# Group softmax on one core: 12 in-place tiles, one DMA ring that alternates store(i) and load(i+10)

## The chip, the cores and the metric

The kernel runs on one core of a Trainium2 chip. The core's engines used here are VectorE (DVE), ScalarE (ACT) and SyncE (SP, which issues the DMAs); TensorE is not used. Times are device microseconds of that core. The metric is the median time of one execution: 1601.17 us before, over three runs (1600.88 to 1601.21).

## What is computed

The input x has the shape (4, 4096, 4352), float32. Each row of 4352 values is cut into 8 groups of 544, and each group is replaced by its softmax.

```python
x_g = x.reshape(B, N, G, Dg)            # G = 8, Dg = 544
x_g = x_g - x_g.max(axis=-1, keepdims=True)
exp = np.exp(x_g)
out = exp / exp.sum(axis=-1, keepdims=True)
```

The whole input is read once from HBM and the whole output is written once: 285.21 MB each way.

## The kernel before

The 16384 rows are taken in 128 tiles of 128 rows, one row to a partition, so a tile is 128 x 4352 float32 values, 2176 KB (17408 bytes in each partition). For each tile the kernel

- loads it into xt with one DMA (line 32, issued by SyncE);
- takes the negated maximum of each of the 8 groups on VectorE (line 35, one reduction over the whole tile, into mx);
- computes the exponentials on ScalarE, one instruction per group (line 40), from xt into a second tile ot, with the group's sum going to a column of sm. The profile shows each as an ACTIVATE and a short ACTIVATION_READ_ACCUMULATOR;
- takes the reciprocals of the 8 sums on VectorE (line 49, into rs);
- multiplies each group by its reciprocal on VectorE (line 51), from ot into ot;
- stores ot with one DMA (line 52, issued by SyncE).

xt and ot come from one pool with bufs=4: four buffers for each of the two names. mx, sm and rs come from a small pool, also with four buffers each. The loop is written tile after tile; the framework schedules the instructions itself, so the order on an engine need not be the written one, and it puts in the semaphore waits. Each engine, and SyncE's queue of DMA issues, works its instructions in order: an instruction that waits holds those behind it on the same engine. All loads and stores are issued by SyncE and go through one DMA queue, q1, in the order of issue.

Of the kernel before, what the change touches and what calls it, by code (L numbers as in the profile page):

```python
# [1 line left out]

# [4 lines left out]


@with_exitstack
def kernel(  # L10
    ctx: ExitStack,
    tc: tile.TileContext,
    x: bass.AP,
    out: bass.AP,
):
    nc = tc.nc
    G = 8
    P = 128
    xf = x.flatten_outer_dims()
    of = out.flatten_outer_dims()  # L20
    N, D = xf.shape
    Dg = D // G
    xg = xf.rearrange("n (g d) -> n g d", g=G)
    og = of.rearrange("n (g d) -> n g d", g=G)
    ntiles = N // P

    pool = ctx.enter_context(tc.tile_pool(name="io", bufs=4))
    small = ctx.enter_context(tc.tile_pool(name="small", bufs=4))

    for t in range(ntiles):  # L30
        xt = pool.tile([P, G, Dg], mybir.dt.float32)
        nc.sync.dma_start(out=xt, in_=xg[t * P:(t + 1) * P])  # L32

        mx = small.tile([P, G], mybir.dt.float32)
        nc.vector.reduce_max(out=mx, in_=xt, axis=mybir.AxisListType.X, negate=True)  # L35

        sm = small.tile([P, G], mybir.dt.float32)
        ot = pool.tile([P, G, Dg], mybir.dt.float32)
        for g in range(G):
            nc.scalar.activation(  # L40
                out=ot[:, g, :],
                in_=xt[:, g, :],
                func=mybir.ActivationFunctionType.Exp,
                bias=mx[:, g:g + 1],
                scale=1.0,
                accum_out=sm[:, g:g + 1],
            )
        rs = small.tile([P, G], mybir.dt.float32)
        nc.vector.reciprocal(out=rs, in_=sm)  # L49
        for g in range(G):  # L50
            nc.vector.tensor_scalar_mul(out=ot[:, g, :], in0=ot[:, g, :], scalar1=rs[:, g:g + 1])  # L51
        nc.sync.dma_start(out=og[t * P:(t + 1) * P], in_=ot)  # L52


# [1 line left out]
_INS = ['x']  # L56
_OUTS = [((4, 4096, 4352), 'float32')]


# [23 lines left out]
```

## Time and profile before

| | |
|---|---|
| median of three runs | 1601.17 us |
| span of the profiled execution | 1599.5 us |
| moved between HBM and SBUF | 285.21 MB read, 285.21 MB written |
| mean over the span | 357 GB/s |
| VectorE busy | 1048.2 us, 66% |
| ScalarE busy | 760.8 us, 48% |
| DMA queue q1, time of its packets as a share of 16 engines' span | 85.6% |

The span runs from the first to the last instruction of the profiled execution; the time of a run lies a little above it. Busy shares are means over the whole span. Where an engine is idle, the profile names what released it, which says what it had been waiting for. SyncE computes nothing; its rows are DMA issues, and the time to landing of a DMA counts from its issue to the last arrival of its completion signals, so it includes the time that the transfer stands in the queue behind others. The rows on which the prediction rests stand in a section of their own below.

### The profile page before, as it was taken

What the parts mean: (1) busy time and instruction counts of PE and PEld (TensorE: products, weight loads), DVE (VectorE), ACT (ScalarE), POOL (GpSimd) and SP (SyncE); (2) the same over time, 40 slices, a digit from 0 to 9 for tenths busy, and PEclk for the clock granted to TensorE, in tenths of its full rate; (3) what the DMA queues carried; (4) which work ended last, traced back from release to release, by engine and by line L of the source; (5) the groups of instructions that cost most, each with busy time, mean ns of one, the idle gap of its engine ahead of it and who ended that gap; (6) DMA issues with size and microseconds to landing.
All of it is one profiled execution on the core that took longest, in us unless ns stands there. A gap on an engine that the chain in (4) does not pass through costs nothing.

```text
span 1599.5 us, 4255 instructions
## 1 busy us (share of the span) xinstructions
DVE 1048.2 (66%) x1280; ACT 760.8 (48%) x2049; POOL 0.2 (0%) x4
## 2 busy tenths in 40 slices
DVE  7568655587556775567765677656776567765566
ACT  6245444455444554445544355443554435544354
POOL 0000000000000000000000000000000000000000
DMA  8888998888988889888898888998889988898887
GB/s 362 355 341 349 376 383 346 337 349 369 390 348 341 349 355 390 361 337 353 351 383 369 341 349 355 374 378 336 344 359 376 376 342 341 362 375 371 344 340 312
DMA packets 36897, 570.71 MB, mean 357 GB/s; under 512 B 4096, under 2 KB 4096, under 8 KB 4096
## 3 DMA queue, kind: packets, MB, share of 16 engines
q1 hardware_dynamic: 36864, 570.44, 85.6%
q14 instruction: 33, 0.27, 0.0%
HBM read 285.21 MB, written 285.21 MB: 357 GB/s over the span
## 4 chain that ended last, share of the span: by engine, by line
DMA 33%; DVE 27%; ACT 26%; issue 10%; SPq 1%; DVEq 0%; ACTq 0%
DMA xt<-in_x_dram 33%; ACT ot L40 26%; DVE ot L51 18%; DVE mx L35 8%; DVE rs L49 1%; SPq L32 1%; SPq L52 1%; DVEq L78 0%; ACTq L78 0%
## 5 line engine op out<-in xcount | busy, mean ns | idle before, releaser
L40 ACT ACTIVATE ot<-xt,mx 128x544 f32<-128x544 f32 x1024 | 750.7, 734 | 817.8 <-DVE mx L35 667.3
L35 DVE TENSOR_REDUCE mx<-xt 128x8 f32<-128x4352 f32 x128 | 599.5, 4683 | 426.0 <-DMA xt<-in_x_dram 426.0
L51 DVE TENSOR_SCALAR ot<-ot,rs 128x544 f32<-128x544 f32 x1024 | 434.3, 499 | 4.5
L40 ACT ACTIVATION_READ_ACCUMULATOR ot<-xt,mx 128x1 f32 x1024 | 191.4, 187 | 0.0
L49 DVE RECIPROCAL rs<-sm 128x8 f32<-128x8 f32 x128 | 25.5, 199 | 113.3 <-ACT ot L40 113.3
L40 ACT ACT_TABLE_LOAD x1 | 1.3, 1283 | 9.7 <-DMA xt<-in_x_dram 9.7
L67 POOL MEMSET const-uint8-127<- 128x1 uint8 x1 | 0.1, 102 | 0.0
L67 POOL MEMSET const-bfloat16-1.0<- 128x1 bf16 x1 | 0.1, 101 | 0.0
L67 POOL MEMSET const-float32-0.0<- 128x1 f32 x1 | 0.1, 98 | 0.2 <-issue 0.2
L67 POOL MEMSET const-float32-1.0<- 128x1 f32 x1 | 0.1, 98 | 0.0
## 6 DMA issues: line engine op xcount, KB each, us to landing
xt<-in_x_dram SPq DMA_DIRECT2D x128, 2176.0 KB, 17.1
out_dram<-ot SPq DMA_DIRECT2D x128, 2176.0 KB, 6.6
```

The source lines that it names most:

```text
L32: nc.sync.dma_start(out=xt, in_=xg[t * P:(t + 1) * P])
L35: nc.vector.reduce_max(out=mx, in_=xt, axis=mybir.AxisListType.X, negate=True)
L40: nc.scalar.activation(out=ot[:, g, :], in_=xt[:, g, :], func=mybir.ActivationFunctionType.Exp, bias=mx[:, g:g + 1], scale=1.0, accum_out= ...
L49: nc.vector.reciprocal(out=rs, in_=sm)
L51: nc.vector.tensor_scalar_mul(out=ot[:, g, :], in0=ot[:, g, :], scalar1=rs[:, g:g + 1])
L52: nc.sync.dma_start(out=og[t * P:(t + 1) * P], in_=ot)
L67: nc = _bacc.Bacc("TRN2", target_bir_lowering=False, num_devices=1)
```

## The change

Three things are changed together. The second tile ot is gone: the exponentials and the multiplies work in place in xt. The pool has 12 buffers of that one tile. And the instructions are issued in the written order on each engine, which is now: ten loads first; then, for each i, the maximum and the exponentials of tile i, the reciprocals and multiplies of tile i-1, the store of tile i-1, and the load of tile i+9. So on SyncE store(j) is followed by load(j+10). With 12 buffers, load(j+10) goes into the buffer that tile j-2 had.

```diff
+    NBUF = 12
-    pool = ctx.enter_context(tc.tile_pool(name="io", bufs=4))
+    pool = ctx.enter_context(tc.tile_pool(name="io", bufs=NBUF))
     small = ctx.enter_context(tc.tile_pool(name="small", bufs=4))
-    for t in range(ntiles):
-        xt = pool.tile([P, G, Dg], mybir.dt.float32)
-        nc.sync.dma_start(out=xt, in_=xg[t * P:(t + 1) * P])
+    def load(i):
+        xt = pool.tile([P, G, Dg], f32, name="xt")
+        tiles[i] = xt
+        nc.sync.dma_start(out=xt, in_=xg[i * P:(i + 1) * P])
+    def store(i, eng):
+        eng.dma_start(out=og[i * P:(i + 1) * P], in_=tiles.pop(i))
+    def expo(i):
+        xt = tiles[i]
+        mx = small.tile([P, G], f32, name="mx")
         nc.vector.reduce_max(out=mx, in_=xt, axis=mybir.AxisListType.X, negate=True)
-        ot = pool.tile([P, G, Dg], mybir.dt.float32)
+        sm = small.tile([P, G], f32, name="sm")
+        sums[i] = sm
         for g in range(G):
             nc.scalar.activation(
-                out=ot[:, g, :],
+                out=xt[:, g, :],
                 in_=xt[:, g, :],
                 func=mybir.ActivationFunctionType.Exp,
                 bias=mx[:, g:g + 1],
                 scale=1.0,
                 accum_out=sm[:, g:g + 1],
             )
+    def scale(i):
+        xt = tiles[i]
+        rs = small.tile([P, G], f32, name="rs")
+        nc.vector.reciprocal(out=rs, in_=sums.pop(i))
         for g in range(G):
-            nc.vector.tensor_scalar_mul(out=ot[:, g, :], in0=ot[:, g, :], scalar1=rs[:, g:g + 1])
-        nc.sync.dma_start(out=og[t * P:(t + 1) * P], in_=ot)
+            nc.vector.tensor_scalar_mul(out=xt[:, g, :], in0=xt[:, g, :], scalar1=rs[:, g:g + 1])
+    AHEAD = NBUF - 2
+    with tc.manual_schedule():
+        for i in range(AHEAD):
+            load(i)
+        for i in range(nt + 1):
+            if i < nt:
+                expo(i)
+            if i:
+                scale(i - 1)
+                store(i - 1, nc.sync)
+                if i - 1 + AHEAD < nt:
+                    load(i - 1 + AHEAD)
```

## Rows read from the trace of the kernel before

**Rows 1.** The page: its first line, the packets' total, and part 3, DMA queue q1.
```profile
span 1599.5 us, 4255 instructions
...
DMA packets 36897, 570.71 MB, mean 357 GB/s; under 512 B 4096, under 2 KB 4096, under 8 KB 4096
...
q1 hardware_dynamic: 36864, 570.44, 85.6%
```

**Rows 2.** Groups by line: line, engine, operation, shapes, count | busy us, mean ns | idle before.
```profile
L40 ACT ACTIVATE ot<-xt,mx 128x544 f32<-128x544 f32 x1024 | 750.7, 734 | 817.8 <-DVE mx L35 667.3 <-issue 150.6
L35 DVE TENSOR_REDUCE mx<-xt 128x8 f32<-128x4352 f32 x128 | 599.5, 4683 | 426.0 <-DMA xt<-in_x_dram 426.0
L51 DVE TENSOR_SCALAR ot<-ot,rs 128x544 f32<-128x544 f32 x1024 | 434.3, 499 | 4.5
...
L49 DVE RECIPROCAL rs<-sm 128x8 f32<-128x8 f32 x128 | 25.5, 199 | 113.3 <-ACT ot L40 113.3
```

**Rows 3.** Waits, all engines: who waited for whom, us in total, times, longest.
```profile
DVE mx L35 <- DMA xt<-in_x_dram: 426.0, 64, 13.2
```

**Rows 4.** Waits of SyncE's queue, same columns.
```profile
SPq L52 <- DVE ot L51: 1397.0, 127, 24.1
```

**Rows 5.** Timeline of SyncE, 100 to 210 us: start, length, line, operation, count.
```profile
108.59 3.96 SPq L32 DMA_DIRECT2D xt<-in_x_dram  x4
135.47 22.77 SPq L52 DMA_DIRECT2D out_dram<-ot  x4
158.33 3.96 SPq L32 DMA_DIRECT2D xt<-in_x_dram  x4
```

**Rows 6.** Windows of 2 us: window, length, engines' busy, PEclk, DMA share, GB/s.
```profile
192.00:194.00 2.00, 2.00 (x5) 2.00 (x7) 0.00 (x0) 1.00 0.00 0
200.00:202.00 2.00, 1.44 (x4) 2.00 (x7) 0.00 (x0) 1.00 0.00 0
206.00:208.00 2.00, 1.61 (x4) 0.00 (x0) 0.00 (x0) 1.00 0.66 279
```

**Rows 7.** Longer windows: one with a turn in 24 us; loads; stores; loads; two turns.
```profile
160.00:184.00 24.00, 11.80 (x9) 8.46 (x23) 0.00 (x0) 1.00 1.01 418
...
166.00:184.00 18.00, 11.80 (x9) 8.46 (x23) 0.00 (x0) 1.00 1.01 431
...
37.40:53.00 15.60, 10.91 (x17) 7.26 (x21) 0.00 (x0) 1.00 1.01 429
4.00:22.00 18.00, 10.94 (x7) 8.88 (x22) 0.00 (x0) 1.00 1.00 428
...
161.00:167.00 6.00, 0.00 (x0) 0.00 (x0) 0.00 (x0) 1.00 0.98 360
...
260.50:266.50 6.00, 0.00 (x0) 0.00 (x0) 0.00 (x0) 1.00 1.00 367
```

**Rows 8.** Issue to landing: page's median store; issues at 0.73, 2.11, 58.47, 111.35 us.
```profile
out_dram<-ot SPq DMA_DIRECT2D x128, 2176.0 KB, 6.6
...
xt<-in_x_dram SPq DMA_DIRECT2D x1, 2176.0 KB, 8.9
...
xt<-in_x_dram SPq DMA_DIRECT2D x1, 2176.0 KB, 23.1
...
out_dram<-ot SPq DMA_DIRECT2D x1, 2176.0 KB, 7.6
...
xt<-in_x_dram SPq DMA_DIRECT2D x1, 2176.0 KB, 25.5
```

**Rows 9.** Timeline of SyncE, single issues: the first four loads, their fourth, a later fourth, the last store.
```profile
0.73 2.80 SPq L32 DMA_DIRECT2D xt<-in_x_dram  x4
2.11 1.42 SPq L32 DMA_DIRECT2D xt<-in_x_dram  x1
111.35 1.20 SPq L32 DMA_DIRECT2D xt<-in_x_dram  x1
1592.08 0.33 SPq L52 DMA_DIRECT2D out_dram<-ot  x1
```

More of the change, by code (lines that the diff above doesn't have):

```diff
@@ L24 @@
     og = of.rearrange("n (g d) -> n g d", g=G)
-    ntiles = N // P
-    pool = ctx.enter_context(tc.tile_pool(name="io", bufs=4))
+    nt = N // P
+    pool = ctx.enter_context(tc.tile_pool(name="io", bufs=NBUF))
     small = ctx.enter_context(tc.tile_pool(name="small", bufs=4))
-    for t in range(ntiles):
-        xt = pool.tile([P, G, Dg], mybir.dt.float32)
-        nc.sync.dma_start(out=xt, in_=xg[t * P:(t + 1) * P])
-        mx = small.tile([P, G], mybir.dt.float32)
+    f32 = mybir.dt.float32
+    tiles = {}
+    sums = {}
+    def load(i):
[7 more added lines that the diff above has]
+        mx = small.tile([P, G], f32, name="mx")
         nc.vector.reduce_max(out=mx, in_=xt, axis=mybir.AxisListType.X, negate=True)
-        sm = small.tile([P, G], mybir.dt.float32)
-        ot = pool.tile([P, G, Dg], mybir.dt.float32)
+        sm = small.tile([P, G], f32, name="sm")
+        sums[i] = sm
         for g in range(G):
             nc.scalar.activation(
-                out=ot[:, g, :],
+                out=xt[:, g, :],
                 in_=xt[:, g, :],
@@ L47 @@
             )
-        rs = small.tile([P, G], mybir.dt.float32)
-        nc.vector.reciprocal(out=rs, in_=sm)
+    def scale(i):
+        xt = tiles[i]
+        rs = small.tile([P, G], f32, name="rs")
+        nc.vector.reciprocal(out=rs, in_=sums.pop(i))
         for g in range(G):
-            nc.vector.tensor_scalar_mul(out=ot[:, g, :], in0=ot[:, g, :], scalar1=rs[:, g:g + 1])
-        nc.sync.dma_start(out=og[t * P:(t + 1) * P], in_=ot)
+            nc.vector.tensor_scalar_mul(out=xt[:, g, :], in0=xt[:, g, :], scalar1=rs[:, g:g + 1])
[11 more added lines that the diff above has]
+                    load(i - 1 + AHEAD)
 _INS = ['x']
```

## The prediction, made before the change was run

> **What bounds the kernel now.** I read the page's totals first. The span is 1599.5 us, 570.7 MB move in it at a mean of 357 GB/s, and the transfers' packets fill 85.6% of the span [rows 1]. No engine is near that: over 128 tiles VectorE needs (599.5 + 434.3 + 25.5)/128 = 8.28 us a tile and ScalarE 750.7/128 = 5.86 us [rows 2], while the kernel takes 1599.5/128 = 12.50 us a tile. So the DMA engines set the pace, and the question is what they do in the 14.4% in which they hold no packet.
>
> Second, who waits. VectorE waits 426.0 us, in 64 waits, for loads [rows 3]: two per group of four tiles. SyncE's queue waits 1397.0 us, in 127 waits, for the multiplies of line 51 [rows 4]. That queue holds everything behind a waiting store, the next loads too, and its timeline shows what this makes: four stores spread over 22.77 us, then four loads together, with a period of 158.33 - 108.59 = 49.74 us for four tiles [rows 5]. While the stores trickle out as VectorE finishes them, nothing else is queued: 0 GB/s in 192 to 194 and in 200 to 202 us, 279 in 206 to 208 [rows 6]. The holes are in the transfer queue, not in its speed.
>
> Third, what the transfers do when something is queued. Loads back to back run at 428 and 431 GB/s (the second with both engines at work), three stores back to back at 429 [rows 7]. A transfer is 2176 KB = 2.228 MB, so a load takes 2.228/431 = 5.17 us and a store 2.228/429 = 5.19 us. One thing costs more: the turn from a store to the load behind it. The 6 us around a turn run at 360 and 367 GB/s; against 430 that loses 6 x 70/430 = 0.98 and 6 x 63/430 = 0.88 us. The 24 us with a turn near its start run at 418 and lose 24 x 12/430 = 0.67 us [rows 7]. The landings agree: a store with loads behind it lands 7.6 us after its issue, the median store after 6.6 [rows 8].
>
> **The change part by part.** *Loads ahead and the ring's order.* Ten loads are issued at once; then SyncE issues store(j), load(j+10) in turn. Load(j+10) takes the buffer of tile j-2, so it waits until store(j-2) has landed. At that moment load(j+8), store(j-1), load(j+9) and store(j) are still queued, some 22 us of transfers. Behind the waiting load on SyncE stands store(j+1), and nobody but the transfer queue waits for these two. An issue takes 0.3 to 1.4 us (1.42 and 1.20 are the slow ones [rows 9]), and even a load on an idle queue lands in 8.9 us [rows 8], so the backlog covers the wait; the holes go.
>
> *The compute order.* scale(i-1) now stands behind max(i) on VectorE, and max(i) waits for load(i). So store(i-1) is ready about 4.7 (max) + 0.2 + 434.3/128 = 3.4, together 8.3 us, after load(i) lands. When load(i) lands, the queue's next store is store(i-9): eight stores, each 10 us or more apart, lie between. This costs nothing as long as VectorE's 8.28 us and ScalarE's 5.86 us a tile [rows 2] stay under a tile's transfer time, below. At the start store(0) is ready at 0.73 + 8.9 [rows 8, 9] + 4.7 + 5.9 + 3.6 = 24 us, and loads keep the queue busy to 56 us. At the end tile 127 needs 4.7 + 5.9 + 3.6 = 14.2 us after its load, and some 50 us of stores stand ahead of its store.
>
> *In place.* ot goes; the exponentials write over xt. No row shows an exponential in place. The nearest is line 51, which already works in place, ot on ot, at 499 ns for 544 columns [rows 2]. I take no change. ScalarE would have to slow from 5.86 to over 11 us a tile before it counted.
>
> *The turns.* This is the unknown. Before, there is one store-to-load turn per four tiles; now there is one per tile, 118 in all, and as many from load to store. For store to load I take 0.9 us, with 0.67 and 1.0 as its ends (three of the four rows lie at 0.88 to 1.0). For load to store the one near thing is a store issued at 135.47, just before the last load of its group landed at 111.35 + 25.5 = 136.85. That store landed at 135.47 + 6.6 = 142.07, 5.22 us behind the load [rows 5, 8, 9]: a store's own 5.19, so the turn cost nothing. I take 0. Its far end is the other turn's 0.9. On the low side both turns could vanish; less than no cost would mean over 431 GB/s, which no long stretch shows.
>
> *The sum, against the profiled span.* The fourth load lands at 2.11 + 23.1 = 25.2 us [rows 8, 9], and six more at 5.17 bring the tenth to 56.2. Then 118 pairs of 5.19 + 5.17 + 0.9 = 11.26 us give 1328.7. Ten last stores at 5.19 give 51.9. The last store's issue at 1592.08 plus 6.6 leaves 0.8 us to the end of the span [rows 8, 9]. Together 1437.6 us. The median of the runs, 1601.17, is 1.7 us above the profiled span, so the forecast is 1439.3. Against the period now: 49.74 us for four tiles becomes 45.0; some 7 us of holes go and three more turns take 2.7 back.
>
> [...]
>
> **The rivals.** *The forecast*: turns of 0.67 to 1.1 us a pair, 1412 to 1463 us (118 x 0.23 = 27 us down, 118 x 0.2 = 24 us up). 0.68.
>
> *Cheaper turns.* With reads and writes queued all the time the DMA engines could drift apart and cover the turns. With none at all a pair is 10.36 us and the time 1333; so 1333 to 1412. Against it: the loads are issued right behind their store (135.47 + 22.77 = 158.24, then 158.33 [rows 5]), some 5 us before the turn comes, and it still costs 0.9. 0.12.
>
> *Turns both ways.* If load to store costs as much as store to load, a pair is 12.16 us and the time 1546; so 1463 to 1546. The one row near it speaks against it. 0.10.
>
> *A ceiling on the mixed rate, no change.* If the mean of now, 357 GB/s, were all that both directions together can have, filling holes would only stretch the transfers: 570.4 MB at 357 GB/s is 1598 us, with the 1.7 about 1599. The long windows at 429 to 431, each in one direction, speak against it; that none is mixed leaves it open. [...] 0.04.
>
> *The queue runs dry, slower.* If the wait of a load falls on the store issued just ahead of it, rather than two stores back, whatever makes it so (the buffer's release, the count of transfers in flight), the change doesn't do what it says. Then the ring is empty whenever a load is issued: a load on an idle queue takes 8.9 us to land [rows 8], the store behind it 5.19, a pair 14.1 us, the time about 1774. It decides from a pair of (1599.5 - 108.9)/118 = 12.63 us on. Against it: the buffer distance of two in the loop, with 22 us of backlog against 8.9. 0.06. [...]
>
> **How the numbers follow.** The likeliest is 1439 us. Its own range is 1412 to 1463. To hold 8 in 10 the range takes the nearer parts of both neighbours, 1385 to 1510 (a turn of 0.45 us a pair at one end, 1.5 at the other), and leaves out the far parts of the neighbours, the ceiling and the dry queue. A difference of 0.2%, 3 us, is about what a measurement of this kernel can tell from none. Faster: 0.68 + 0.12 + 0.10 = 0.90; same 0.04; slower 0.06.
>
> **What the profile after would show.** DMA packets over 95% of the span and no 2 us window without bytes between 3 us and the end; a mean near 397 GB/s; SyncE's queue waiting for landings of stores where it now waits for line 51; a store landing about every 11.3 us. If the holes are gone and the period is 10.4 or 12.2 instead, the turns are mis-sized; at 12.5 with full packets the ceiling holds. Holes behind each store, with loads landing 9 us after issue, would make the step on the wait wrong. Exponentials well over 734 ns, or multiplies over 499, would make the in-place step wrong.

## The result, and the profile after

The changed kernel takes 1341.13 us (median, 1340.14 to 1341.88) against 1601.15 for the kernel before: a ratio of 0.8376, 95% interval 0.8364 to 0.8388. The forecast was 1439 with a range of 1385 to 1510. The direction was right, the gain was 260 us where 162 were forecast, and the time lies below the range, beside the low end (1333) of the rival "cheaper turns", which had 0.12.

The page of the changed kernel: its first line, the engines' busy times, the packets' total, and the DMA queue (compare [rows 1]).

```profile
span 1340.1 us, 4119 instructions
...
DVE 1046.7 (78%) x1280; ACT 764.3 (57%) x2049; POOL 0.2 (0%) x4
...
DMA packets 36896, 570.70 MB, mean 426 GB/s; under 512 B 4096, under 2 KB 4096, under 8 KB 4096
...
q1 hardware_dynamic: 36864, 570.44, 99.4%
q14 instruction: 32, 0.26, 0.0%
```

The same bytes fill 99.4% of the span instead of 85.6%. The busy times of VectorE and ScalarE are those of before. By these shares the time without a packet falls from 230 us to 8, and the time of the packets themselves from 1369 us to 1332: of the 259 us that the span lost, some 222 are holes and some 37 are packets that now take less time. The groups by line (compare [rows 2]) and SyncE's queue (compare [rows 4]) of the changed kernel:

```profile
L49 ACT ACTIVATE xt<-xt,mx 128x544 f32<-128x544 f32 x1024 | 751.2, 735 | 524.3 <-issue 435.8
L45 DVE TENSOR_REDUCE mx<-xt 128x8 f32<-128x4352 f32 x128 | 599.6, 4685 | 247.6 <-DMA xt<-in_x_dram 247.6
L63 DVE TENSOR_SCALAR xt<-xt,rs 128x544 f32<-128x544 f32 x1024 | 434.2, 498 | 4.5
...
SPq L37 <- DMA out_dram<-xt: 1104.5, 116, 16.7
```

Working in place costs nothing: 735 ns against 734, 498 against 499. SyncE now waits 1104.5 us, in 116 waits, at a load (line 37) for the landing of a store, where it used to wait 1397.0 us at a store for VectorE. The timeline of its issues in mid-run (start, length, operation):

```profile
499.26 0.33 SPq L37 DMA_DIRECT2D xt<-in_x_dram  x1
499.64 0.48 SPq L40 DMA_DIRECT2D out_dram<-xt  x1
509.55 0.33 SPq L37 DMA_DIRECT2D xt<-in_x_dram  x1
```

A pair takes 10.29 us here. That is less than the forecast's 11.26, and no more than the 10.36 that a load of 5.17 and a store of 5.19 need with no turn between them. Windows of the changed kernel say the same (window, length, engines' busy, PEclk, DMA share, GB/s): the first turn from the ten loads to the stores, the stretch behind it, mid-run, and the end.

```profile
52.00:58.00 6.00, 5.96 (x11) 4.73 (x13) 0.00 (x0) 1.00 0.99 408
...
56.00:62.00 6.00, 5.96 (x6) 3.83 (x11) 0.00 (x0) 1.00 1.02 437
...
400.00:600.00 200.00, 157.38 (x191) 114.14 (x308) 0.00 (x0) 1.00 1.01 431
...
1300.00:1325.00 25.00, 2.17 (x6) 0.00 (x0) 0.00 (x0) 1.00 1.00 428
1325.00:1330.00 5.00, 0.00 (x0) 0.00 (x0) 0.00 (x0) 1.00 0.24 101
1330.00:1335.00 5.00, 0.00 (x0) 0.00 (x0) 0.00 (x0) 1.00 0.19 80
1335.00:1340.00 5.00, 0.00 (x0) 0.00 (x0) 0.00 (x0) 1.00 0.08 35
```

Only the first turn shows: 408 against 431 over 6 us is 0.3 us. Windows this short swing by some packets (56 to 62 us has 437, 62 to 68 has 418). The completion signals agree: every transfer here sends sixteen (the 4096 packets under 512 B, for 256 transfers), which I read as one from each of the sixteen DMA engines; the records do not name the engine. By the median of the sixteen the tenth load and the first store together took 10.7 us, and the next two pairs 10.4 and 10.3. From the second turn on a mixed stream runs at 430 to 431 GB/s, the rate of loads alone in [rows 7]. And there is an end that the prediction had not: from 1326 us on only four of the sixteen DMA engines still work, three of them until 1335, the last until 1339.

So two questions stand: why a turn that cost 0.9 us before costs nothing now, and which parts of the change bring the gain.

### The profile page after: what moved, and what is told of

The parts are those of the page before. It is cut to its first block, busy times and chain, and to the rows that moved or that the text cites. A ratio compares the mean times of both kernels' runs of the same rounds, so it can differ in the third digit from the quotient of the medians.

```text
span 1340.1 us, 4119 instructions
## 1 busy us (share of the span) xinstructions
DVE 1046.7 (78%) x1280; ACT 764.3 (57%) x2049; POOL 0.2 (0%) x4
## 2 busy tenths in 40 slices
DMA packets 36896, 570.70 MB, mean 426 GB/s; under 512 B 4096, under 2 KB 4096, under 8 KB 4096
## 3 DMA queue, kind: packets, MB, share of 16 engines
q1 hardware_dynamic: 36864, 570.44, 99.4%
## 4 chain that ended last, share of the span: by engine, by line
DMA 88%; DVE 7%; SPq 1%; ACT 1%; issue 1%; DVEq 0%; ACTq 0%
DMA out_dram<-xt 85%; DVE mx L45 4%; DVE xt L63 3%; DMA xt<-in_x_dram 3%; SPq L37 1%; ACT xt L49 1%; DVE rs L61 0%; DVEq L104 0%; ACTq L104 0%
## 5 line engine op out<-in xcount | busy, mean ns | idle before, releaser
L49 ACT ACTIVATE xt<-xt,mx 128x544 f32<-128x544 f32 x1024 | 751.2, 735 | 524.3 <-issue 435.8
L63 DVE TENSOR_SCALAR xt<-xt,rs 128x544 f32<-128x544 f32 x1024 | 434.2, 498 | 4.5
L49 ACT ACTIVATION_READ_ACCUMULATOR xt<-xt,mx 128x1 f32 x1024 | 191.3, 187 | 0.0
```

The costliest lines, as they stand in the source:

```text
L49: nc.scalar.activation(out=xt[:, g, :], in_=xt[:, g, :], func=mybir.ActivationFunctionType.Exp, bias=mx[:, g:g + 1], scale=1.0, accum_out= ...
L63: nc.vector.tensor_scalar_mul(out=xt[:, g, :], in0=xt[:, g, :], scalar1=rs[:, g:g + 1])
```

## What a turn is paid for: bursts on an empty queue

**e1.** Nothing is computed. Bursts of transfers, ten of each kind, are issued on an empty queue; a VectorE copy of one column holds back the next burst until all of the last has landed.

S is the store of a tile, L the load of one, S40 a store of 40 of a tile's 128 rows, put in front to set the DMA engines out of step; that it does so was my assumption. A kind of burst is a row of these: S S L is two stores and a load. One kind of burst, as an example (the other kinds are left out here):

```diff
...
+        for k in range(REPS):              # S S L
+            st(a)
+            st(c)
+            ld(b)
+            touch(c, b)
+            touch(a, b)
...
```

> No softmax here: only bursts of transfers of one tile each (2176 KB), ten of a kind, each burst issued on an empty queue after the one before has landed (one VectorE column holds it back). [...] The question is why a store-to-load turn cost 0.9 us in the kernel before and nothing in the changed one. Read from the landing of the store just ahead of a load, against the same store with no load behind it. All theories: S lands after 6.6 us, in S L after 7.6. Theory 1, reading ahead: the price is the start of reading from HBM, paid by the first load after the queue was empty, not by each turn: in S S L the second store lands 1.0 later than in S S; in L S L the store lands as in L S, within 0.2; in S40 S L 1.0 later than in S40 S. Theory 2, a lead in the queue: a load that stands queued for more than one transfer ahead costs nothing: S S L as S S, L S L as L S, S40 S L 1.0 later. Theory 3, engines in step: the turn costs because all sixteen turn at once: S S L and L S L each 1.0 later, S40 S L at most 0.5 later.

The timeline of SyncE, first issue of the first and of the tenth burst of each kind, in the order S; S L; S S; S S L; L S; L S L; S40 S; S40 S L; L:

```profile
25.34 0.35 SPq L45 DMA_DIRECT2D out_dram<-a  x1
86.92 0.33 SPq L45 DMA_DIRECT2D out_dram<-a  x1
...
93.77 0.33 SPq L45 DMA_DIRECT2D out_dram<-a  x1
210.98 0.33 SPq L45 DMA_DIRECT2D out_dram<-a  x1
...
224.00 0.33 SPq L45 DMA_DIRECT2D out_dram<-a  x1
334.56 0.33 SPq L45 DMA_DIRECT2D out_dram<-a  x1
...
346.73 0.33 SPq L45 DMA_DIRECT2D out_dram<-a  x1
511.82 0.33 SPq L45 DMA_DIRECT2D out_dram<-a  x1
...
530.29 0.34 SPq L40 DMA_DIRECT2D b<-in_x_dram  x1
669.54 0.33 SPq L40 DMA_DIRECT2D b<-in_x_dram  x1
...
685.46 0.33 SPq L40 DMA_DIRECT2D b<-in_x_dram  x1
870.24 0.33 SPq L40 DMA_DIRECT2D b<-in_x_dram  x1
...
891.26 0.38 SPq L49 DMA_DIRECT2D out_dram<-e  x1
1003.18 0.31 SPq L49 DMA_DIRECT2D out_dram<-e  x1
...
1015.61 0.31 SPq L49 DMA_DIRECT2D out_dram<-e  x1
1182.39 0.31 SPq L49 DMA_DIRECT2D out_dram<-e  x1
...
1200.85 0.34 SPq L40 DMA_DIRECT2D b<-in_x_dram  x1
1280.06 0.33 SPq L40 DMA_DIRECT2D b<-in_x_dram  x1
```

A ninth of each difference is the time of one burst: 6.84, 13.02, 12.28, 18.34, 15.47, 20.53, 12.44, 18.53 and 8.80 us. The load at the end adds 6.18 us to S, 6.06 to S S, and 5.06 to L S. It needs 5.17 in a full queue. So after S and after S S the turn costs 0.9 to 1.0 us, and after L S it costs nothing, though the same store stands ahead of it. With the store of 40 rows in front, the load adds 18.53 - 12.44 = 6.09 us: the price is there, too. By the last of each transfer's completion signals, counted from the end of the burst's first issue: the store lands after 6.21 us in S and 7.16 in S L, the second store after 11.43 in S S and 12.39 in S S L; in S40 S L it lands as in S40 S (11.72 and 11.67) and the load pays instead. The 40 rows, 31% of a tile's bytes, hold the store behind them up about as long as a whole tile does (11.72 against 11.43); no run shows how they are spread over the engines.

A lead in the queue (theory 2) falls with S S L, where the load is queued some 10 us ahead of its turn. Engines in step (theory 3) falls with L S L; the 6.09 us of S40 S L speak against it only if the 40 rows do set the engines apart. Theory 1 meets all but two points: in S40 S L the price shows at the load and not at the store, and it had no price for L S. A store adds 15.47 - 8.80 = 6.67 us to a lone load (whose burst takes 8.80), about 1.5 more than its 5.19. The turn from load to store has a price too, if it is the first. About 1.0 of this 1.5 is on all engines: by the median of its sixteen signals the load lands after 7.1 us alone and after 8.1 with a store behind it. The rest is one engine that falls further behind the others, 1.1 us alone and 1.6 with the store.

**e5.** Longer bursts, in the same way: how does the price grow with the number of turns?

```diff
...
+            for t in (b, c, d):        # S L S L S L
+                st(a)
+                ld(t)
...
```

> Again no softmax, only bursts on an empty queue, ten of a kind: S L S L S L; L S L S L S; S L L S S L. In e1 a burst paid about 1.0 us at its first turn when it began with a store (S L and S S L) and 1.5 us when it began with a load (L S), and the second turn of L S L cost nothing. Theory 1, restated: the turn is paid once after the queue was empty, at the first change of direction, and not again while something is queued. S L S L S L: the last load lands at 7.16 + 5 x 5.17 = 33.0 us after the first issue; L S L S L S: the last store at 14.94 + 4 x 5.17 = 35.6; S L L S S L: 33.0. Theory 3 restated (each turn from store to load costs while the engines are in step): two more turns at 1.0: 35.0, 37.6, and 34.0.

The last landing came 34.8, 36.7 and 34.4 us after the first issue (counted as in e1). Neither theory gave these numbers: one turn paid gave 33.0, 35.6 and 33.0, each turn from store to load 35.0, 37.6 and 34.0. The first issues of the first and of the tenth burst S L S L S L:

```profile
25.25 0.35 SPq L45 DMA_DIRECT2D out_dram<-a  x1
345.47 0.34 SPq L45 DMA_DIRECT2D out_dram<-a  x1
```

The bursts follow each other every 35.58, 37.22 and 35.51 us (from (345.47 - 25.25)/9 and likewise). Six transfers without any turn would be 6.84 + 5 x 5.18 = 32.7, or 34.7 with a load first. So five turns cost 2.8, five turns 2.5, and three turns 2.8 us. The price does not grow with the turns. Taken apart by the landings of S L S L S L, against 6.21 and 5.18 more for each transfer, the excess is 1.1 us at the first store (7.3), 2.2 at the first load (13.6), 2.4 at the second store (19.0), then 2.6 to 2.7: here the first turn of each direction pays about 1.1, the later three together 0.4. In a burst that begins with a load it is not so: the first turn pays 1.5, the turn from store to load behind it nothing (L S L, above), and the later three of L S L S L S together about 1.0.

That is the answer to the first question, as far as the runs go: after the queue was empty, the first turn costs 0.9 to 1.5 us, the second 1.1 or nothing, and the next ones little; in a queue that stays full they cost nothing (431 GB/s, 10.29 us a pair). That engines drift apart is not needed for this: from 60 to 120 us of the changed kernel thirteen of the sixteen signals of each transfer come within 0.6 us, less than one packet's 0.65, and the rate is 430 GB/s. The kernel before emptied its queue in every period of four tiles and so paid in every period; I took this for the price of a turn. What makes up that price no run shows.

## Keeping the queue full: the distance between a store and the load that waits for it

```diff
-    AHEAD = NBUF - 2
+    AHEAD = NBUF          # e2; NBUF - 1 in e3
```

**e2.** Each load waits for the store just issued.

> The changed kernel with twelve loads ahead in place of ten, so that load(j+12) takes the buffer of the store just issued and each pair starts on an empty queue: the dry queue of the prediction, made on purpose. The prediction's price: a load lands 8.9 us after its issue, a pair takes 14.1 us, 1774 us in all. [...]

```profile
xt<-in_x_dram SPq DMA_DIRECT2D x128, 2176.0 KB, 10.3
out_dram<-xt SPq DMA_DIRECT2D x128, 2176.0 KB, 15.1
```

1891.99 us: the dry queue is real, slower than the kernel before, and its price was too low. A pair takes (1890.2 - 24 x 5.2)/116 = 15.2 us, against 14.1. By these rows of its page (median from issue to landing) a load lands 10.3 us after its issue and the store behind it 15.1: it is the burst L S of e1 (15.47 us) over and over, with both a lone load's start and the first turn in each. The prediction had taken 8.9, the landing of the first load of the kernel, and no turn.

**e3.** Each load waits for the store before that one.

> The changed kernel with eleven loads ahead: load(j+11) waits for the store one before the one just issued, so about two transfers, 10.4 us, stay queued. If any backlog that covers a landing and an issue is enough, the time stays within 0.5% of 1341 us. If the cheap turn needs a load queued two or more transfers ahead (theory 2), turns of up to 0.9 us come back: up to 1341 + 117 x 0.9 = 1446 us.

1379.26 us, in between. The windows of this kernel tell when:

```profile
400.00:500.00 100.00, 78.12 (x100) 59.15 (x159) 0.00 (x0) 1.00 1.01 431
600.00:700.00 100.00, 77.06 (x99) 57.01 (x153) 0.00 (x0) 1.00 1.00 412
900.00:1000.00 100.00, 73.69 (x90) 52.94 (x143) 0.00 (x0) 1.00 1.00 400
```

One pair of backlog is enough for some 600 us and then not. My reading is that some DMA engines fall behind. All sixteen must land a store before the load that waits for it is issued (from store(0) on, the changed kernel issues load(j+12) 0.02 to 0.10 us after the sixteenth signal of store(j), up to 3.6 us after the fifteenth); so the others eat up their backlog of 10.4 us while they wait for the slowest, their queues run low, and turns cost again. By the completion signals, the slowest engine was 5.5 us behind the mean of the other fifteen at 552 us and 6.9 at 595, when the rate fell (the expectation of e12 below has 4 to 5 us for this, which is too low).

Part of what may put them behind is in the records of single packets of the changed kernel. The instruction fetches (queue q14, 8 KB, 0.31 us) start at 57.9, 105.9 and 161.0 us, for instance; at 58.2, 106.2 and 161.3 a packet of q1 starts that takes 1.12, 0.95 to 1.06 and 1.00 us in place of 0.65. All 32 have such a packet right behind them, of 0.75 to 1.18 us; with the fetches' own 0.31 us that makes 19 us. In the kernel before, which has holes in every period, the engines stay together: its stores land with all sixteen signals within 0.2 us (median). In the changed kernel's stream without holes the delays add up: at the end four engines are 13.6, 12.7, 10.2 and 3.1 us behind the last of the other twelve, about 40 us together. So my estimate from these numbers is that the fetches account for about half of it, if all of them fell on these four, which the records do not show. One engine, for instance, fell from 4.2 to 6.3 us behind between 701 and 1062 us in steps of less than 0.1 us, which is no fetch; what makes the other half no run shows.

**e12.** The distance of e3 with fewer instructions to fetch (those of e11, below).

> The kernel of e11 (fewer instructions to fetch) with the distance of e3 (load(j+11) waits for the store one before the one just issued). In e3 the rate stayed at 430 GB/s until about 570 us and fell to 400 and less from then on. If the falling behind of the DMA engines that also fetch instructions is the reason (a landing counts only when the slowest engine has landed, while the others eat their backlog), then the fall begins when that lag reaches the same 4 to 5 us: it grew to 13.7 us at the end of the changed kernel and to 9.3 in e11, so at about 570 x 13.7/9.3 = 840 us, and the time is about 1336 + 24 = 1360 us. If the shorter backlog alone is the reason, the fall begins at the same 570 us and the time is about 1374 us.

1335.54 us: no fall at all, 429 to 434 GB/s in every slice from the eighth to the last but one (the page's 40 slices of the span):

```profile
GB/s 399 425 429 427 429 429 428 433 431 429 434 431 430 433 430 431 433 430 431 433 431 430 433 431 430 432 432 430 433 431 431 432 433 429 432 433 429 432 433 343
```

The slowest engine came to be at most 5.7 us behind the mean of the others, and never the 6.9 at which the rate of e3 fell. This goes the way that the late engines' theory says and against a backlog that is too short by itself, but my estimate of the onset (840 us) failed, and the kernel of e11 has other work on its engines as well; so the threshold is not settled.

**e4.** Six buffers and four loads ahead, the distance still two.

```diff
-    NBUF = 12
+    NBUF = 6
```

> The changed kernel with 6 buffers and 4 loads ahead; load(j+4) still waits for store(j-2). If the distance of two keeps the queue full and the number of buffers is not what matters, 1341 us within 0.5%: a store is ready 13.5 us after its turn to be issued comes, against 20 us queued. If the depth of loads ahead matters (compute late for its store), the queue runs empty in each pair and the time is 1400 us or more.

1354.22 us, 1.0% above the changed kernel where 0.5% was expected. The middle runs at the same 430 to 432 GB/s. What is lost lies at the start (371 and 410 GB/s in the first two slices against 399 and 426: four loads do not last until the first store is ready) and in the last six slices (418, 395 and 391 before the last). SyncE waits at the stores for VectorE here (1206.7 us in 128 waits), so the margin is gone. The signals show late engines there too (the slowest 10.4 us behind the median at 1170 us and 12.2 at 1255), which would eat it at the end; no run separates the two.

## Which part of the change brings the gain

**e6.** The in-place step undone: xt and ot again, six buffers each.

```diff
-    NBUF = 12
+    NBUF = 6
+        ot = pool.tile([P, G, Dg], f32, name="ot")
+        tiles[i] = ot
-                out=xt[:, g, :],
+                out=ot[:, g, :],
-    AHEAD = NBUF - 2
+    AHEAD = NBUF - 1
```

> The written order kept, the in-place step undone: six buffers of xt and six of ot in place of twelve of one tile, five loads ahead. A load no longer waits for a store at all (its buffer is free after the exponentials); the exponentials of tile i wait for store(i-6). If the queue stays full, as theory 1 needs and no more, 1341 to 1355 us (a few us more at the start, where only five loads are ahead). If working in place is what gains, 1400 us or more.

1340.46 us: the same time, with ot. Working in place is not needed. (A load here takes the buffer of a tile whose exponentials are done; the stores wait for VectorE, 1199.9 us in 128 waits, and the queue stays full.)

**e7.** The kernel before with more buffers alone.

```diff
-    pool = ctx.enter_context(tc.tile_pool(name="io", bufs=4))
+    pool = ctx.enter_context(tc.tile_pool(name="io", bufs=6))
```

> The kernel before with one number changed: bufs=6 in place of 4, so twelve tiles as in the changed kernel, but with ot and in the framework's own order. If the number of buffers is what gains, near 1341 us. If the order on SyncE's queue is what counts (stores held back in a group, then loads in a group), the holes stay in each group, now of six tiles: 6 loads, then 6 stores; the period keeps about 7.3 us of holes and one turn per group, (6 x 10.36 + 7.3 + 0.9)/6 = 11.7 us a tile, about 1500 us.

1601.91 us: no change, and not the 1500 expected. The timeline of SyncE in this kernel shows the same groups of four, 49.7 us apart, as [rows 5]:

```profile
108.33 3.95 SPq L32 DMA_DIRECT2D xt<-in_x_dram  x4
135.16 22.76 SPq L52 DMA_DIRECT2D out_dram<-ot  x4
158.01 3.95 SPq L32 DMA_DIRECT2D xt<-in_x_dram  x4
```

So the order of issue does not change, and the two further buffers of each do nothing for it. That the small pool's four buffers hold the group at four is likely, and was not tried.

**e9.** The changed kernel's source order without the step that makes the engines issue in it.

```diff
-    with tc.manual_schedule():
+    if True:
```

> The changed kernel without the step that makes the engines issue in written order: the same source order, in place, 12 buffers, but the framework schedules. SyncE's list of issues comes out the same (store(j), load(j+10) in turn); VectorE's does not: the multiplies of one tile are mixed with other work. If only SyncE's order and the loads ahead count, 1341 us within 0.5%, with a DMA share over 99%. If the written order of the compute engines is part of the gain, over 1355.

1698.64 us: the second case of the expectation, and far beyond it, slower than the kernel before. SyncE's list is the same, but its stores come 13.5 to 13.9 us apart, because VectorE and ScalarE now take turns. The timeline of one tile (start, length, engine, line, operation, count, idle before and what ended it):

```profile
600.10 4.68 DVE L45 TENSOR_REDUCE mx<-xt 128x8 f32<-128x4352 f32 x1
...
604.86 0.75 ACT L49 ACTIVATE xt<-xt,mx 128x544 f32<-128x544 f32 x1 [7.93 <-issue]
605.22 0.34 SPq L40 DMA_DIRECT2D out_dram<-xt  x1
...
610.86 0.20 DVE L61 RECIPROCAL rs<-sm 128x8 f32<-128x8 f32 x1 [5.67 <-ACT xt L49]
611.09 2.57 DVE L63 TENSOR_SCALAR xt<-xt,rs 128x544 f32<-128x544 f32 x6
613.58 4.68 DVE L45 TENSOR_REDUCE mx<-xt 128x8 f32<-128x4352 f32 x1
...
619.10 0.34 SPq L40 DMA_DIRECT2D out_dram<-xt  x1
```

The next maximum stands behind six of the eight multiplies, not ahead of the reciprocals; so ScalarE waits 7.9 us for a maximum (the row says issue, but the exponentials start 0.1 us after the maximum has ended at 604.78), VectorE 5.7 us for the exponentials, and a tile takes 4.7 + 5.9 + 0.2 + 2.6 = 13.4 us and more. With max(i) written ahead of scale(i-1), the two overlap and need 8.28 us a tile. So SyncE's order with the loads ahead gains nothing here without the order on VectorE. The reverse, VectorE's order without SyncE's, was not tried.

## The end, and a faster version

**e8.** Can the last stores be kept off the late engines? That stores of 104 and of 24 rows leave some engines out, and the late ones among them, was my assumption.

```diff
...
+            eng.dma_start(out=og[i * P:i * P + 104], in_=xt[:104])
+            eng.dma_start(out=og[i * P + 104:(i + 1) * P], in_=xt[104:])
```

> The changed kernel with the stores of the last two tiles each split in 104 and 24 rows. [...]

1350.28 us, ratio 0.8436 (0.8422 to 0.845): 9 us slower than the changed kernel, where a gain was hoped for. Which engines the two pieces go to no run shows, so how much of the 9 us is more work on the late ones is open. Part of it may be in packets that took longer: some between 1316 and 1333 us took up to 2.8 us in place of 0.65, where from 1300 us on none of the changed kernel took over 0.66; why, no run shows.

In the expectation of e10 I read the late landings as three engines 13.7, 8.5 and 3.2 us behind. They are the last three landings of one engine, in steps of 5.17 us; the late engines are the four above, 13.6, 12.7, 10.2 and 3.1 us behind. So the ratio to the instruction counts, on which e10 and e11 were built, was a misreading. What the two runs measured stands without it.

**e10.** One multiply in place of eight.

```diff
-        for g in range(G):
-            nc.vector.tensor_scalar_mul(out=xt[:, g, :], in0=xt[:, g, :], scalar1=rs[:, g:g + 1])
+        nc.vector.tensor_mul(out=xt, in0=xt, in1=rs.unsqueeze(2).to_broadcast([P, G, Dg]))
```

> The changed kernel with the eight multiplies of a tile as one VectorE instruction: 896 of 4119 instructions less. In the changed kernel thirteen DMA engines end at 1325 us and three late, by 13.7, 8.5 and 3.2 us, close to the ratio of the instructions of ScalarE (2049) and VectorE (1280): each engine's instruction fetches (8 KB each) seem to run on one DMA engine of their own. If so, the end does not move (ScalarE's fetches set it): 1341 us within 0.15%, and only the second late engine comes in earlier, by about 6 us, so the landings at 1330 and 1333 to 1336 us fall to about 1328. If all fetches share the late engines alike, 32 fetches become 25 and the end moves 3 us: 1338. VectorE's busy time rises to 9 or 10 us a tile and stays under the 10.35 of the transfers.

1341.9 us (1339.55 to 1342.52), ratio 0.8379 (0.8365 to 0.8393): no change in the end, 26 fetches in place of 32. The last DMA engine is still 14.1 us late, the second and third 7.1 and 3.4; so six fetches fewer did not bring the last one in. The single multiply takes 4692 ns where the eight took 434.2/128 = 3.39 us, and VectorE is busy 90% of the span, still without effect.

**e11.** ScalarE's sums moved to VectorE, the multiplies to GpSimd.

```diff
-                accum_out=sm[:, g:g + 1],
...
-        nc.vector.reciprocal(out=rs, in_=sums.pop(i))
-        for g in range(G):
-            nc.vector.tensor_scalar_mul(out=xt[:, g, :], in0=xt[:, g, :], scalar1=rs[:, g:g + 1])
+        sm = sums.pop(i)
+        nc.vector.reduce_sum(out=sm, in_=xt, axis=mybir.AxisListType.X)
+        nc.vector.reciprocal(out=rs, in_=sm)
+        nc.gpsimd.tensor_mul(out=xt, in0=xt, in1=rs.unsqueeze(2).to_broadcast([P, G, Dg]))
```

> The changed kernel with ScalarE's sums taken off it: no accumulator reads (1024 instructions fewer on ScalarE), the 8 sums by one VectorE reduction, the multiplies by one GpSimd instruction. The same result is computed. ScalarE keeps 1025 instructions, VectorE 384, GpSimd about 130. If each engine's fetches delay one DMA engine, the last engine ends 6.9 us after the thirteen in place of 13.7: about 1334 us, ratio 0.995 to the changed kernel. VectorE is then busy 9.6 us of 10.33 a tile. The risk is GpSimd, of which no row here has a price: over 10.3 us a tile its multiply becomes the bound, and the time is 128 times it.

1336.25 us (1335.82 to 1337.46), ratio 0.835 (0.8337 to 0.8362) to the kernel before, 0.4% below the changed kernel; the two intervals just do not meet. From its page:

```profile
DVE 1208.2 (90%) x384; ACT 669.8 (50%) x1025; POOL 952.8 (71%) x132
...
q14 instruction: 21, 0.16, 0.0%
...
L63 POOL TENSOR_TENSOR xt<-xt,rs 128x4352 f32<-128x4352 f32 x128 | 952.6, 7442 | 354.8 <-DVE rs L62 312.5
```

With 21 fetches the last landing comes at 1334.9 us in place of 1339.3, and that is what the time gained: 4.4 of 4.9 us. That fewer fetches made it so is likely and not shown: with 26 of them (e10) nothing was gained. GpSimd's multiply takes 7.4 us of the 10.33 that a tile's transfers take. Which instruction stream's fetches go to which DMA engine is open.

## Why the prediction was wrong, and where it was right

*The bound and the holes: right.* Transfers set the pace, the holes were 14.4% of the span (230 us, or 7.2 a group, where the prediction has some 7), and they are gone: 99.4% against the 95% asked for.

*The wait for store(j-2): right*, and with less room than the 22 us of backlog suggested: at a distance of one the queue holds for some 600 us only (e3), at none it is the dry queue (e2).

*In place: right* (735 and 498 ns), and by e6 of no account at all. *The compute order: right* in that it costs nothing; that an order like it is needed (e9) the prediction did not see.

*The turns: the step that failed.* I priced 118 turns at 0.9 us, 106 us, from windows around turns in [rows 7] and one landing in [rows 8]. Each was the first turn after a hole. Rows that are alike in this can't give the price of a turn in a full queue, and I took their agreement for evidence. The pair measures 4.456 MB at 431 GB/s, 10.34 us, against 11.26; the prediction had named 10.4 as the sign that the turns were mis-sized. The turn from store to load, a term of 0.9 us in the sum, measures nothing in a queue that is kept full. The sum with that value, 56.2 + 118 x 10.34 + 51.9 + 0.8, is 1329 us of span.

*Load to store:* the zero that I read from [rows 5, 8, 9] was right for the full queue by luck, for its ground was wrong. I set a store's landing against the landing of the load ahead of it; a turn delays the transfer ahead of it (S in S L lands 1.0 later), so that difference hides its price. L S against L shows it. The row misled in a second way: I took the last of the load's sixteen signals, which came 0.5 us behind the median one. By the medians the store landed 5.6 us behind the load (141.95 against 136.4), so 0.4 us of a turn did stand in that row.

*The end: missed.* The measured span is 1340.1, 11 us over that sum. The prediction let all sixteen DMA engines end together. The slowest engine's 13.6 us at the end are new; in the kernel before, with its holes, a store's sixteen signals come within 0.2 us (median). The two errors have opposite signs: 118 x 0.92 = 109 us too much for the turns, 11 too little for the end.

*The rivals.* "Cheaper turns" was the right one, though its ground (engines that drift apart) is not what the runs show: at 60 to 120 us of the changed kernel thirteen engines are in step, within 0.6 us, and the price is not there (430 GB/s). The ceiling falls: 431 GB/s mixed in mid-run, and 426 over the whole span. The dry queue decides where it was said to, but at 1892 us instead of 1774.

## What to carry to other kernels

A price read beside a stall belongs to the stall until a row shows it without one: ask of every row whether the queue had just been empty, and of a transfer's price whether it shows at the transfer ahead. When a queue is to be kept full, write both orders down, that of the issues and that of the engine that releases them: here the first without the second came out slower than the kernel before (1698.64 us in e9 against 1600.55). Leave more backlog than one landing needs: here 10.4 us, against 8.9 for the landing of a lone load, held for some 600 us only (e3), my reading being that the slowest of the sixteen DMA engines counts, which was 5.5 us behind the mean of the others at 552 us and 6.9 at 595.

## What the hardware showed that I had not expected

Loads and stores in turn run at 431 GB/s on one core, as fast as loads alone, with 0.65 us for nearly every packet of 17408 bytes. After an empty queue the first turn costs 0.9 to 1.5 us, and five turns in a burst (2.8 and 2.5 us) cost no more than three (2.8). A burst of one load takes 2.0 us longer than one of a store (8.80 against 6.84). In the changed kernel's stream without holes DMA engines fell behind each other by up to 13.6 us in 1340, 1% of the time; thirty-two instruction fetches of 8 KB, 0.05% of the bytes, account by my estimate above for about half of the delay.
